# Second layer's attention: TensorE's order written out in the source instead of found by the planner

## The chip, the cores and the metric

The kernel runs on one core of one Trainium2 chip. The core has five engines that run side by side, each through its own list of instructions in order: TensorE (PE in the profile; matmuls, results in PSUM), VectorE (DVE), ScalarE (ACT), GpSimd (POOL) and SyncE (SP, which only issues DMA transfers here). They wait for each other through semaphores. The metric is the device time of one execution in microseconds; less is better. Before the change it was 1603.55 us (median of 3 runs, 1603.0 to 1605.21).

## The reference: what is computed

Two transformer layers over 512 latent tokens and 256 context tokens of width 1024, in float32. The change touches the attention of the second layer, where only the latent tokens are still updated:

```python
h_x = modulate(rmsnorm(x, norm_g[1, 0]), shift, scale);  h_c = ...            # 512 x 1024, 256 x 1024
q_x, k_x, v_x = split(h_x @ w_in_c, [1024, 1280])      # 16 query heads of 64, 4 key and value heads
k_c, v_c      = split(h_c @ w_in_c[:, 1024:], 2)
q_x, k_x      = rope(q_x), rope(k_x)
# each block of 128 queries sees 256 context keys and the latent keys within 128 positions:
s = q @ k.T / 8, masked;  p = softmax([s, sink])[..., :-1];  o = p @ v        # sink: one learned logit per head
x = x + gate * (o @ w_out_c)                                                   # 1024 x 1024
```

After it come the norm and the SwiGLU feed-forward part of the layer, and the last norm.

## The kernel before

**Layout.** Activations lie with features on the 128 partitions and tokens along the free axis: eight tiles `hb[k]` (views `hx` for the 512 latent, `hc` for the 256 context tokens). Every float32 product is made of three fast ones: each operand is split into a high and a low part (`split`, L196 and L197), and `mm3` (L207 to L209) issues high x high, high x low and low x high for each of the `KT` = 8 blocks of the contraction, 24 matmuls of 512 columns for a projection of 128 outputs.

**Weights** come through `Stream` (`S`): SP loads a 512 KB tile, ScalarE makes its high part (L158), VectorE its low part (L159). `S.next()` hands out the next in a fixed order and asks for those after it; there are three buffers of each kind.

**The stage.** Its PSUM pools are two buffers of two banks for scores (`sps`, tile `s`), one bank for projections (`linp`, tile `lin`) and three banks for everything else (`tp`, tile `t`). First come keys 0 (`k_x(0)`), the norm of the context (`rstd_of`, `h_make`), the values (`v_part`, matmuls L432 to L434 of 256 columns), context keys and keys 1, then query tile 0 (`q_piece(0)`). A query tile goes through `q_tile`: `rope_of` reads the projection's bank twice on VectorE (L386, L387) and works twice on POOL (L388, L389), then `evac_pair` splits it on ScalarE and VectorE (L369, L372).

**The steps.** There are 32, `gqa_step(m, i)`: head pair `m` (0 to 7), block of 128 queries `i` (0 to 3). Part `a` issues the scores of both heads against context and latent keys (L1540, L1542; 512 keys for `i` 0 and 3, 640 for 1 and 2), then for each head the mask with the row's minimum on VectorE (L1544), the exponential on ScalarE (L1549, L1551), the reciprocal of the sum on VectorE (L1553, L1554) and the scaling on POOL (L1557). Part `b` turns the probabilities on TensorE (L1569, L1581: 8 or 10 transposes of 128 x 128), copies them out of PSUM (L1577 ScalarE, L1575 VectorE, L1582 ScalarE) and, at every second step, multiplies them with the values for two query blocks at once (`values`, L411, 20 to 24 matmuls) and splits the result into the place where the output projection reads it.

**Fillers.** `run_steps` (L439) traces a step's `a`, the last step's `b`, then that step's fillers: whole query projections (`q_piece`, 24 matmuls) and first halves of the output projection (`first_part`, 12 matmuls per 128 outputs, over head pairs 0 to 3), listed by `plan` (L1636). After the 32 steps, `wo1` adds the second halves.

**What sets the order.** The source order is not the order on the engines. A planner runs the traced instructions through a timeline of its own at build time, and puts on each engine's list the instruction that is ready first by that timeline, with the source order as priority; at run time each list is worked off in order. `high_priority` and `issue_after` in `unbroken` (L396) keep one group of matmuls together as far as the planner lets them.

Of the kernel before, what the change touches and what calls it, by code (L numbers as in the profile page):

```python
# [11 lines left out]
ALU = mybir.AluOpType  # L12
# [5 lines left out]
KT = D // P  # L18
NX = 512
# [18 lines left out]
def tile_trunk(  # L38
# [27 lines left out]
    nc = tc.nc  # L66
# [138 lines left out]
    def mm3(ps, wh, wl, xh, xl, n=KT):  # L205
        for k in range(n):
            nc.tensor.matmul(ps, wh(k), xh(k), start=k == 0, stop=False)  # L207
            nc.tensor.matmul(ps, wh(k), xl(k), start=False, stop=False)  # L208
            end = nc.tensor.matmul(ps, wl(k), xh(k), start=False, stop=k == n - 1)  # L209
        return end  # L210
# [1242 lines left out]
    with ExitStack() as st:  # L1453
# [18 lines left out]
        def q_tile(m, ps):  # L1472
            qs[m] = gp.tile([P, 2, NX], F32R, tag="gq", name="gq", bufs=4)
            evac_pair(qs[m], 0, NX, rope_of(ps, gp), -0.125)


        def k_x(i, w):
            ps = tp()
            mm3(ps, *w, xh, xl)
            evac_pair(k1[:, 2 * i : 2 * i + 2, :], NC, NX, rope_of(ps, gp), 1.0)  # L1480
# [7 lines left out]
        def v_part(g, w):  # L1488
            ps = tp((P, 2, 256))
            v_group(ps, g, w)  # L1490
            nc.scalar.copy(v[:, 2 * g : 2 * g + 2, :], ps)

        w0 = [wslice(t) for t in S.next()]
        k_x(0, w0)
        r = rstd_of(linp(), c_sums, D, npool)
# [29 lines left out]
        def gqa_step(m, i):  # L1525
            kv = m // 2
            lo, hi = max(i - 1, 0), min(i + 1, 3)
            nk = (hi - lo + 1) * P
            d = {}

            def a():
                q = qs[m]
                small = lambda name: gp.tile([P, 2], F32, tag=name, name=name, bufs=4)
                mx, rs, es = small("mx"), small("rs"), small("es")
                pp = []
                for c in range(2):
                    ql = q[:, c, i * P : (i + 1) * P]
                    s = sps.tile([P, 1024], F32, tag="s", name="s")
                    for n, k in ((0, k1), (1, k2)):
                        nc.tensor.matmul(s[:, 256:512], ql, k[:, kv, 0:NC], start=(n == 0), stop=(n == 1))  # L1540
# [3 lines left out]
                    nc.vector.tensor_tensor_reduce(  # L1544
                        out=sv, in0=sv, in1=gm0 if i == 0 else gm[:, 0 : 256 + nk], op0=ALU.add, op1=ALU.min,
                        scale=1.0, scalar=snk[:, 2 * m + c : 2 * m + c + 1], accum_out=mx[:, c : c + 1],
                    )
                    p = gp.tile([P, 640], F32, tag="p", name="p", bufs=5)
                    nc.scalar.activation(p[:, 0 : 256 + nk], sv, AF.Exp, bias=mx[:, c : c + 1], scale=-1.0, accum_out=rs[:, c : c + 1])  # L1549
# [3 lines left out]
                nc.vector.tensor_add(rs, rs, es)  # L1553
                nc.vector.reciprocal(rs, rs)  # L1554
                for c in range(2):
                    z = pp[c][:, 0 : 256 + nk]
                    nc.gpsimd.tensor_scalar(z, z, rs[:, c : c + 1], 1.0, op0=ALU.mult, op1=ALU.mult)  # L1557
                d["p"] = pp

            def b():  # L1560
                nb = 2 + hi - lo + 1
                h = i % 2
                if h == 0:
                    turned[0] = gp.tile([P, 2, 10, P], F32, tag="pt", name="pt", bufs=1)
                pt = turned[0]
                for c in range(2):
                    t = tp((P, 4, P))
                    for k in range(4):
                        nc.tensor.transpose(t[:, k, :], d["p"][c][:, k * P : (k + 1) * P], ident)  # L1569
                    if i == 0:  # L1570
                        z, t = pt[:, c, 0:6, :].rearrange("p (a b) n -> p a b n", b=3)[:, :, 0:2, :], t.rearrange("p (a b) n -> p a b n", b=2)
                    else:
                        z = pt[:, c, 5 * h : 5 * h + 4, :]
                    if c:
                        nc.vector.tensor_copy(z, t)  # L1575
                    else:
                        nc.scalar.copy(z, t)  # L1577
# [24 lines left out]
            return a, b  # L1602


        x1 = {}

        def wo1(m, w, c0, n, k0):
            wh, wl = wo_slices(w, m % 2)
            ps = tp() if k0 else linp()
            cs = slice(c0, c0 + n)  # L1610
            if k0:
                before[0] = mm3(ps[:, 0:n], wh, wl, lambda k: hx[k0 + k][:, 0, cs], lambda k: hx[k0 + k][:, 1, cs], 4)
            else:
                mm3(ps.rearrange("p (a n) -> p a n", a=2), wh, wl, lambda k: att(k)[0], lambda k: att(k)[1], 4)
            gate = mod[1][:, 2, 0, m : m + 1]
            if k0 == 0:
                x1[m] = xr[m]
            nc.vector.scalar_tensor_tensor(x1[m][:, cs], ps[:, 0:n], gate, x1[m][:, cs], op0=ALU.mult, op1=ALU.add)

        def first_part(t):  # L1620
            d = {}

            def f(m):
                if m % 2 == 0:
                    d["w"] = S.next()
                wo1(m, d["w"], 0, NX, 0)

            return [lambda m=m: f(m) for m in (2 * t, 2 * t + 1)]

        for m in range(KT):  # L1630
            S.add(wo_c[m])
        spool = []
        super_weights(1, type("", (), {"tile": lambda self, *a, **k: spool[0].tile(*a, **k)})())
        q_piece(0)()
        steps, fillers = [], []
        plan = {  # L1636
            0: [q_piece(1), q_piece(2)], 1: [q_piece(3), q_piece(4)], 2: [q_piece(5)], 3: [q_piece(6)], 4: [q_piece(7)],
            5: first_part(0), 6: first_part(1) + first_part(2), 7: first_part(3),
        }
        for m in range(8):  # L1640
            steps += [gqa_step(m, i) for i in range(4)]
            fillers += spread(plan[m], 4)
        run_steps(steps, fillers)
        held = []
        for t in range(4):
            w = S.next(0 if t >= 2 else 2)
            for m in (2 * t, 2 * t + 1):
                if t == 0:
                    wo1(m, w, 0, NX, 4)
                else:  # L1650
                    wo1(m, w, 0, 256, 4)
                    held.append((m, w))


        halves = [slice(0, 256), slice(256, 512)]
        sums = sq_sum([x1[k][:, halves[0]] for k in range(KT)], npool)
        for m, w in held[:1]:
            wo1(m, w, 256, 256, 4)
        r = rstd_of(tp(), sums, D, npool)
        for k in range(KT):  # L1660
            h_make(k, hc[k], x1[k][:, halves[0]], r, 1, 1, 0, npool)
        for m, w in held[1:]:
            wo1(m, w, 256, 256, 4)
# [319 lines left out]
```

## Time and profile before

| | |
|---|---|
| median of 3 runs | 1603.55 us |
| span of the profiled execution | 1606.8 us |
| TensorE busy in the span | 1541.8 us (96%), 9854 matmuls |
| VectorE, ScalarE, POOL busy | 1242.9 (77%), 734.1 (46%), 275.9 (17%) us |
| HBM traffic over the span | 103 GB/s |

Times within the execution are counted from the span's start. The stage of the change begins near 990 us and hands over to the feed-forward part near 1240 us. A row of the timeline gives start, duration, engine, line, operation, output and inputs, shape and count, and in square brackets the idle time of the engine just before and what ended it. The duration of a matmul holds its way through the array, so successive ones overlap, and the distance of their starts is what one costs. In rows of windows each engine's busy time is followed by its number of instructions; behind the last engine stand the granted clock of TensorE (1.00 is full speed), the share of the DMA engines and the GB/s they moved. In rows of groups stand busy time, mean duration in ns, and the idle time before them with what ended it.

### The profile page before, as it was taken

What the parts mean: (1) busy time and instruction counts of PE and PEld (TensorE: products, weight loads), DVE (VectorE), ACT (ScalarE), POOL (GpSimd) and SP (SyncE); (2) the same over time, 40 slices, a digit from 0 to 9 for tenths busy, and PEclk for the clock granted to TensorE, in tenths of its full rate; (3) what the DMA queues carried; (4) which work ended last, traced back from release to release, by engine and by line L of the source; (5) the groups of instructions that cost most, each with busy time, mean ns of one, the idle gap of its engine ahead of it and who ended that gap; (6) DMA issues with size and microseconds to landing.
All of it is one profiled execution on the core that took longest, in us unless ns stands there. A gap on an engine that the chain in (4) does not pass through costs nothing.

```text
span 1606.8 us, 25479 instructions
## 1 busy us (share of the span) xinstructions
PE 1541.8 (96%) x9854; PEld 1377.4 (86%) x9854; DVE 1242.9 (77%) x2125; ACT 734.1 (46%) x1276; POOL 275.9 (17%) x311
## 2 busy tenths in 40 slices
PE   5899999999999999999999999999998999999997
PEld 3798888877878998999999998886777899989897
DVE  4667798966698789879798867677766987869686
ACT  4346545445344413434424254466664543525354
POOL 2222223463010000010100001354331000000001
PEclk9999999999999999999999999999999999999999
DMA  9312354543145465485866652320011442423321
GB/s 348 100 53 70 99 157 136 182 128 101 63 132 158 118 173 155 133 221 154 213 183 162 201 146 71 106 66 27 15 40 54 131 144 68 131 72 100 118 80 53
DMA packets 68577, 195.28 MB, mean 122 GB/s; under 512 B 6772, under 2 KB 19220, under 8 KB 68456
## 3 DMA queue, kind: packets, MB, share of 16 engines
q1 hardware_dynamic: 58824, 161.26, 31.5%
q0 software_dynamic: 9056, 31.87, 9.4%
q8 instruction: 78, 1.28, 0.3%
q10 hardware_dynamic: 576, 0.52, 0.1%
q14 instruction: 43, 0.35, 0.1%
HBM read 160.45 MB, written 4.86 MB: 103 GB/s over the span
## 4 chain that ended last, share of the span: by engine, by line
PE 52%; DVE 5%; DMA 4%; issue 4%; ACT 1%; POOL 0%; DVEq 0%; POOLq 0%; ACTq 0%; SPq 0%
PE f L1764 4%; PE f L1763 4%; PE f L1762 4%; PE f L1334 4%; PE f L1333 4%; PE f L1332 4%; PE f L1374 3%; PE f L1375 3%; PE f L1373 3%; PE t L411 2%; PE f L1815 2%; PE f L1817 2%; PE f L1816 2%; DMA wl<-raw 2%; PE t L1569 2%
## 5 line engine op out<-in xcount | busy, mean ns | idle before, releaser
L196 ACT ACTIVATE wh<-raw 128x1024 fp32r<-128x1024 f32 (+1 forms) x96 | 92.3, 978 | 232.4 <-DVE raw L540 106.6
L207 PE MATMUL lin<-hb,wh 128*128 128x512 f32 (+1 forms) x456 | 162.1, 356 | 8.3 <-DVE rbuf L387 2.1
L208 PE MATMUL lin<-hb,wh 128*128 128x512 f32 (+1 forms) x456 | 160.3, 351 | 1.0 <-DVE hb L1106 0.7
L209 PE MATMUL lin<-hb,wl 128*128 128x512 f32 (+1 forms) x456 | 158.4, 347 | 0.0
L197 DVE TENSOR_TENSOR wl<-raw,wh 128x1024 fp32r<-128x1024 f32 (+1 forms) x96 | 107.1, 1122 | 36.3 <-ACT wh L196 34.3
L269 DVE SCALAR_TENSOR_TENSOR junk<-raw,tables 128x1024 bf16<-128x1024 f32 x80 | 98.6, 1233 | 19.2 <-DMA raw<-in_ada_wT_dram 18.7
L202 POOL DMA_DIRECT2D wl<-raw x39 | 34.0, 872 | 445.3 <-ACT wl L201 412.0
L207 PEld LDWEIGHTS lin<-hb,wh 128*128 128x128 f32 x456 | 86.3, 189 | 23.9 <-issue 2.8
L1373 PE MATMUL f<-g,wh 128*128 128x512 f32 (+1 forms) x304 | 103.0, 340 | 0.6 <-DVE s L1362 0.6
L1374 PE MATMUL f<-g,wh 128*128 128x512 f32 (+1 forms) x304 | 102.9, 339 | 0.0
L1763 PE MATMUL f<-hb,wh 128*128 128x256 f32 x360 | 101.8, 284 | 0.0
L1762 PE MATMUL f<-hb,wh 128*128 128x256 f32 x360 | 101.6, 283 | 0.0
L1764 PE MATMUL f<-hb,wl 128*128 128x256 f32 x360 | 101.4, 284 | 0.0
L1375 PE MATMUL f<-g,wl 128*128 128x256 f32 (+1 forms) x304 | 100.8, 337 | 0.0
L1334 PE MATMUL f<-hb,wl 128*128 128x384 f32 x288 | 96.5, 335 | 1.0 <-DMA wl<-raw 1.0
L208 PEld LDWEIGHTS lin<-hb,wh 128*128 128x128 f32 x456 | 86.5, 190 | 12.4 <-DVE hb L1106 1.4
L159 DVE TENSOR_TENSOR wl<-raw,wh 128x1024 fp32r<-128x1024 f32 x61 | 80.7, 1325 | 20.6 <-ACT wh L158 20.3
L1332 PE MATMUL f<-hb,wh 128*128 128x384 f32 x288 | 96.4, 335 | 0.0
L1333 PE MATMUL f<-hb,wh 128*128 128x384 f32 x288 | 96.4, 335 | 0.0
L209 PEld LDWEIGHTS lin<-hb,wl 128*128 128x128 f32 x456 | 86.5, 190 | 10.8
L158 ACT CAST wh<-raw 128x1024 fp32r<-128x1024 f32 x61 | 63.9, 1048 | 67.0 <-PE t L208 15.0
L339 POOL TENSOR_TENSOR ns_a<-ns_a,ns_s 128x256 f32<-128x256 f32 (+1 forms) x16 | 17.9, 1118 | 433.7 <-ACT ns_s L335 427.0
(395 smaller groups left out, 4851.3 us busy)
## 6 DMA issues: line engine op xcount, KB each, us to landing
raw<-in_w_dram SPq DMA_DIRECT2D x132, 512.0 KB, 3.7
raw<-in_ada_wT_dram SPq DMA_DIRECT2D x80, 512.0 KB, 3.8
wl<-raw POOLq DMA_DIRECT2D x39, 512.0 KB, 6.3
raw<-in_w_ab_dram SPq DMA_DIRECT2D x24, 512.0 KB, 4.2
raw<-in_ada_w_dram SPq DMA_DIRECT2D x16, 512.0 KB, 9.5
raw<-in_w_c_dram SPq DMA_DIRECT2D x12, 512.0 KB, 4.4
nb<-in_na_bias_dram POOLq DMA_DIRECT2D x16, 256.0 KB, 3.2
raw<-in_wo_ab_dram SPq DMA_DIRECT2D x8, 512.0 KB, 3.7
```

Source lines behind the costliest of these rows:

```text
L207: nc.tensor.matmul(ps, wh(k), xh(k), start=k == 0, stop=False)
L208: nc.tensor.matmul(ps, wh(k), xl(k), start=False, stop=False)
L209: end = nc.tensor.matmul(ps, wl(k), xh(k), start=False, stop=k == n - 1)
L1332: nc.tensor.matmul(ps, wh(k), b[:, 0, :], start=k == 0, stop=False)
L1333: nc.tensor.matmul(ps, wh(k), b[:, 1, :], start=False, stop=False)
L1334: nc.tensor.matmul(ps, wl(k), b[:, 0, :], start=False, stop=k == 3)
L1373: nc.tensor.matmul(ps, hi, g[:, 0, cols[v]], start=first, stop=False)
L1374: nc.tensor.matmul(ps, hi, g[:, 1, cols[v]], start=False, stop=False)
L1375: nc.tensor.matmul(ps, lo, g[:, 0, cols[v]], start=False, stop=last)
L1762: nc.tensor.matmul(ps, wh(k), b[:, 0, :], start=k == 0, stop=False)
L1763: nc.tensor.matmul(ps, wh(k), b[:, 1, :], start=False, stop=False)
L1764: nc.tensor.matmul(ps, wl(k), b[:, 0, :], start=False, stop=k == 3)
```

## The change

From ahead of `k_x(0)` until after the squares for the next norm, TensorE's instructions are put on its list in the order of the source; the other engines' lists are still made by the planner. The source order is rewritten for it. A projection is cut into parts that keep one PSUM bank between them: a query tile into 3 + 3 + 2 of its 8 blocks (9, 9 and 6 matmuls), a first half of the output projection into 2 + 2 of its 4 (6 matmuls each). That makes 21 parts of queries 1 to 7, spread over steps 0 to 17, and 16 of the output projection, spread over steps 18 to 31: one part per step, two at steps 0, 6, 12, 18 and 25. Part `b` of a step is divided into turnings (`b`) and values (`b2`). For step n the order is: its scores, the turnings of step n - 1, the filler part, the values of step n - 1 (if it is an odd one). Query tile 0 is still whole and stands directly ahead of the first scores. `wo1` loses its two cases; what it computes is the same.

```diff
+        def in_parts(begin, ps, h, l, cuts, done, cols=slice(0, NX), n=KT):
+            d = {}
+            def f(c):
+                if c == 0:
+                    d["w"], d["ps"] = begin(), ps()
+                o, (wh, wl) = d["ps"][:, cols], d["w"]
+                for k in range(cuts[c], cuts[c + 1]):
+                    nc.tensor.matmul(o, wh(k), h(k), start=k == 0, stop=False)
+                    nc.tensor.matmul(o, wh(k), l(k), start=False, stop=False)
+                    nc.tensor.matmul(o, wl(k), h(k), start=False, stop=k == n - 1)
+                if c == len(cuts) - 2:
+                    done(d["ps"])
+            return [lambda c=c: f(c) for c in range(len(cuts) - 1)]
...
+        by_hand = st.enter_context(ExitStack())
+        by_hand.enter_context(tc.manual_schedule(engines={mybir.EngineType.PE}))
         w0 = [wslice(t) for t in S.next()]
         k_x(0, w0)
         r = rstd_of(linp(), c_sums, D, npool)
...
         def q_piece(m):
-            def f():
-                wh, wl = (wslice(t) for t in S.next())
-                ps = linp() if m else tp()
-                mm3(ps, wh, wl, xh, xl)
-                q_tile(m, ps)
-            return f
+            return in_parts(
+                lambda: [wslice(t) for t in S.next()], linp if m else tp, xh, xl, (0, 3, 6, KT), lambda ps: q_tile(m, ps)
+            )
...
                     nc.scalar.copy(pt[:, :, 5 * h + 4, :], t[:, 0:2, :])
+
+            def b2():
+                h = i % 2
                 if h == 0:
                     return
+                pt = turned[0]
                 o = tp()
...
-            return a, b
+            return a, b, b2
...
+            return [
+                f for m in (2 * t, 2 * t + 1)
+                for f in in_parts(
+                    lambda m=m: begin(m), lambda: linp().rearrange("p (a n) -> p a n", a=2),
+                    lambda k: att(k)[0], lambda k: att(k)[1], (0, 2, 4), lambda ps, m=m: done(m, ps), slice(0, 2), 4,
+                )
+            ]
...
-        q_piece(0)()
-        steps, fillers = [], []
-        plan = {
-            0: [q_piece(1), q_piece(2)], 1: [q_piece(3), q_piece(4)], 2: [q_piece(5)], 3: [q_piece(6)], 4: [q_piece(7)],
-            5: first_part(0), 6: first_part(1) + first_part(2), 7: first_part(3),
-        }
-        for m in range(8):
-            steps += [gqa_step(m, i) for i in range(4)]
-            fillers += spread(plan[m], 4)
-        run_steps(steps, fillers)
+        for f in q_piece(0):
+            f()
+        steps = [gqa_step(m, i) for m in range(8) for i in range(4)]
+
+        fillers = spread([f for m in range(1, 8) for f in q_piece(m)], 18) + spread([f for t in range(4) for f in first_part(t)], 14)
+        for n, (a, b, b2) in enumerate(steps + [(lambda: None,) * 3]):
+            a()
+            if n:
+                steps[n - 1][1]()
+            for f in fillers[n] if n < len(fillers) else []:
+                f()
+            if n:
+                steps[n - 1][2]()
...
         sums = sq_sum([x1[k][:, halves[0]] for k in range(KT)], npool)
+        by_hand.close()
         for m, w in held[:1]:
```

More of the change, by code (lines that the diff above doesn't have):

```diff
@@ L1600, in b, with add_x1, wo1, begin @@
                 split(*(z[:, i // 2, :] for z in att(m)), o[:, both])
-            return a, b
+            return a, b, b2
         x1 = {}
-        def wo1(m, w, c0, n, k0):
+        def add_x1(m, cs, ps):
+            gate = mod[1][:, 2, 0, m : m + 1]
+            nc.vector.scalar_tensor_tensor(x1[m][:, cs], ps, gate, x1[m][:, cs], op0=ALU.mult, op1=ALU.add)
+        def wo1(m, w, c0, n):
             wh, wl = wo_slices(w, m % 2)
-            ps = tp() if k0 else linp()
+            ps = tp()
             cs = slice(c0, c0 + n)
[L1611 to L1618, printed above, removed]
+            before[0] = mm3(ps[:, 0:n], wh, wl, lambda k: hx[4 + k][:, 0, cs], lambda k: hx[4 + k][:, 1, cs], 4)
+            add_x1(m, cs, ps[:, 0:n])
         def first_part(t):
             d = {}
-            def f(m):
+            def begin(m):
                 if m % 2 == 0:
                     d["w"] = S.next()
-                wo1(m, d["w"], 0, NX, 0)
-            return [lambda m=m: f(m) for m in (2 * t, 2 * t + 1)]
+                return wo_slices(d["w"], m % 2)
+            def done(m, ps):
+                x1[m] = xr[m]
+                add_x1(m, slice(0, NX), ps.rearrange("p a n -> p (a n)"))
+            return [
[5 more added lines that the diff above has]
+            ]
         for m in range(KT):
@@ L1648, in tile_trunk @@
                 if t == 0:
-                    wo1(m, w, 0, NX, 4)
+                    wo1(m, w, 0, NX)
                 else:
-                    wo1(m, w, 0, 256, 4)
+                    wo1(m, w, 0, 256)
                     held.append((m, w))
@@ L1656, in tile_trunk @@
         sums = sq_sum([x1[k][:, halves[0]] for k in range(KT)], npool)
+        by_hand.close()
         for m, w in held[:1]:
-            wo1(m, w, 256, 256, 4)
+            wo1(m, w, 256, 256)
         r = rstd_of(tp(), sums, D, npool)
@@ L1662, in tile_trunk @@
         for m, w in held[1:]:
-            wo1(m, w, 256, 256, 4)
+            wo1(m, w, 256, 256)
         nmap = PoolMap(
```

## The prediction

> **What bounds the kernel now.** I read the page first, then the engines' busy time by stages, the groups of TensorE instructions in the stage of the second attention, and then single instructions of that stage in order of time.
>
> ```profile
> span 1606.8 us, 25479 instructions
> PE 1541.8 (96%) x9854; PEld 1377.4 (86%) x9854; DVE 1242.9 (77%) x2125; ACT 734.1 (46%) x1276; POOL 275.9 (17%) x311
> ```
>
> TensorE (PE) is busy 96% of the span, so only what keeps it waiting, or slows its clock, can be won. The next rows are stretches of the stage; after the four engines' busy times comes the granted clock.
>
> ```profile
> 992.00:994.00 2.00, 2.00 (x10) 1.86 (x9) 2.00 (x4) 1.07 (x2) 0.00 (x0) 0.59 0.22 86
> ...
> 1098.00:1102.00 4.00, 1.76 (x10) 1.07 (x8) 3.94 (x11) 3.31 (x9) 1.28 (x1) 0.95 0.00 0
> 1102.00:1106.00 4.00, 3.69 (x12) 2.89 (x13) 3.29 (x9) 1.78 (x7) 3.43 (x3) 0.50 0.43 126
> ...
> 1142.00:1188.00 46.00, 46.00 (x309) 37.36 (x308) 32.20 (x71) 26.15 (x67) 15.49 (x18) 1.00 0.12 35
> ...
> 1030.00:1216.63 186.63, 175.96 (x1145) 139.51 (x1143) 134.28 (x304) 113.65 (x285) 77.58 (x80) 0.98 0.14 42
> ```
>
> In the stage TensorE idles 186.63 - 175.96 = 10.7 us. From 1142 to 1188, where projection work is still at hand, it idles not at all; from 1098 to 1102, where the list of pieces has a hole, it is busy for 1.76 of 4 us, and the four microseconds after run at half clock. Who ends these waits is in the groups:
>
> ```profile
> L1540 PE MATMUL s<-gk,gq 128*128 128x256 f32 x128 | 30.2, 319 | 7.9 <-ACT p L1549 7.3 <-DVE gq L372 0.5
> L1569 PE MATMUL t<-ident,p 128*128 128x128 f32 x256 | 35.8, 281 | 0.4 <-POOL p L1557 0.2
> ```
>
> 7.3 us are scores (L1540) that wait for a PSUM buffer which the exponential (ACT, L1549) still reads. The turnings (L1569) wait for almost nothing: the planner put projection work ahead of them.
>
> **The change part by part.** No instruction is added or dropped; 1145 matmuls of the stage get a new order. Times below are those of the profiled execution; its span of 1606.8 us is 3.2 us above the median of the runs, 1603.55 us, and I add the difference found to the median. The loads of projection weights stay in their order on SP's queue, one tile in about 14 us, with DMA engines at a share of 0.14: I cost them at nothing, and they would cost up to one landing, some 4 us, if a tile were asked for too late. POOL issues no DMA here.
>
> *Step 1, the head.* The block starts ahead of the first key projection.
>
> ```profile
> 990.39 0.51 PE L207 MATMUL t<-hb,wh 128*128 128x512 f32 x1 [1.49 <-ACT hb L354]
> 994.96 1.43 PE L312 MATMUL lin<-res,ones 128*128 128x256 f32 x4
> 998.11 0.42 DVE L317 TENSOR_SCALAR ns_v<-lin 128x256 f32<-128x256 f32 x1
> 999.03 0.40 PE L207 MATMUL t<-hb,wh 128*128 128x512 f32 x1
> 999.27 0.40 PE L432 MATMUL t<-wh,hb 128*128 128x256 f32 x2
> 999.50 0.40 PE L208 MATMUL t<-hb,wh 128*128 128x512 f32 x1
> 1001.76 0.75 DVE L355 SCALAR_TENSOR_TENSOR hb<-norm,mod,hb 128x512 fp32r<-128x512 f32 x1
> 1024.95 0.28 PE L207 MATMUL t<-hb,wh 128*128 128x256 f32 x1
> 1027.82 0.40 PE L207 MATMUL t<-hb,wh 128*128 128x512 f32 x1
> 1033.29 0.39 PE L207 MATMUL lin<-hb,wh 128*128 128x512 f32 x1
> 1038.50 0.39 PE L209 MATMUL lin<-hb,wl 128*128 128x512 f32 x1
> 1039.37 0.51 PE L1540 MATMUL s<-gk,gq 128*128 128x256 f32 x2 [0.48 <-DVE gq L372]
> ```
>
> VectorE delivers the eight normalised tiles hb one by one, the last at 1001.76 + 0.75 = 1002.5. Today value matmuls (L432 to L434) run between those of the key projection (L207 to L209). In source order the key projection comes alone: its 24 matmuls, at (1038.50 - 1033.29) / 23 = 0.227 us each, need 5.4 us and are stretched over the 12 us of deliveries. The context's norm (L312, L317 and two like it of 0.42 us on VectorE) moves behind, which can bring the last tile 1.3 us sooner: 1001.2. Then TensorE still owes 3 matmuls (0.7), the norm's four (1.1), 144 value and 48 context-key matmuls at (1027.82 - 1024.95) / 24 = 0.12 us (23.0), and the second key and first query projection (10.9): 35.7 us, so query 0 ends at 1036.9, not 1033.29: +3.7. Half-idle TensorE loses its clock: after the 1.49 us of idle at 990 it ran four microseconds at a mean of 0.58, which is 1.7 us lost. Paid at the end of this head, it makes +5.4. Bounds: 2.7 (a further 1 us off the deliveries, no clock lost) to 6.7 (no tile sooner).
>
> *Step 2, the first scores.* They need query 0 turned and split (VectorE, POOL, ScalarE, VectorE): 1039.37 - 1033.29 = 6.1 us today, under which query 1 ran, 5.4 us.
>
> ```profile
> 1027.44 1.29 POOL L389 TENSOR_TENSOR rt<-rt,ru 128x512 f32<-128x512 f32 x1
> 1035.78 2.15 POOL L389 TENSOR_TENSOR rt<-rt,ru 128x512 f32<-128x512 f32 x1
> ```
>
> Source order has nothing to put there: query 1's parts stand behind the scores, so TensorE waits bare. POOL's addition took 2.15 us there and 1.29 elsewhere, so the wait is 5.2 to 6.1; I take 5.6. The first scores start 4.9 us later than today (5.4 - 0.5), query 1's 5.4 us are still owed, and the clock is lost again (1.7). Head in all: **+12.0** (7.2 to 13.8).
>
> *Step 3, what is removed.* From the first scores to the output projection's first matmul pass 1216.56 - 1039.37 = 177.2 us. The regular stretch gives the work itself, starts being differences of rows:
>
> ```profile
> 1163.46 1.09 PE L1569 MATMUL t<-ident,p 128*128 128x128 f32 x8
> 1164.31 0.48 PE L1540 MATMUL s<-gk,gq 128*128 128x256 f32 x2
> 1165.57 0.39 PE L207 MATMUL lin<-hb,wh 128*128 128x512 f32 x1
> 1168.33 1.04 PE L1569 MATMUL t<-ident,p 128*128 128x128 f32 x8
> 1169.34 0.48 PE L1540 MATMUL s<-gk,gq 128*128 128x256 f32 x2
> 1170.38 0.40 PE L207 MATMUL lin<-hb,wh 128*128 128x512 f32 x1
> 1173.22 2.17 PE L411 MATMUL t<-pt,gv 128*64 128x256 f32 x20
> 1175.32 1.09 PE L1569 MATMUL t<-ident,p 128*128 128x128 f32 x8
> ...
> 1216.56 0.51 PE L207 MATMUL t<-hb,wh 128*128 128x512 f32 x1
> ```
>
> Turnings 0.85 or 1.01, scores 1.26 (640 keys) or 1.04 (512), a dozen projection matmuls 2.80, values 2.10. For 32 steps: 29.8 + 36.8 + 16 x 2.10 + 20 x 2.80 = 156.2 us. What is over, **-21.0**, is idle time, half clock and small waits; at least the 10 us of shown idle and 2 at half clock should go (-12).
>
> *Step 4, what is late next.* The 7.3 us on ScalarE's buffers go, since turnings and a piece now stand between two scores. In exchange the turnings of a step come right behind the next scores, with the piece behind them. One step's way through softmax:
>
> ```profile
> 1173.46 2.42 POOL L1557 TENSOR_SCALAR p<-p,rs 128x512 f32<-128x512 f32 x2 [2.35 <-DVE rs L1554]
> ...
> 1188.03 0.48 PE L1540 MATMUL s<-gk,gq 128*128 128x256 f32 x2
> 1188.91 0.88 DVE L1544 CUSTOM_DVE_ANT_0 s<-s,gm,snk 128x640 f32<-128x640 f32 x1
> 1189.92 0.59 ACT L1577 COPY pt<-t 128x512 f32<-128x512 f32 x1 [1.41 <-PE t L1569]
> 1190.40 0.80 ACT L1549 ACTIVATE p<-s,mx 128x640 f32<-128x640 f32 x1
> 1191.62 0.81 ACT L1549 ACTIVATE p<-s,mx 128x640 f32<-128x640 f32 x1
> 1192.91 0.15 DVE L1553 TENSOR_TENSOR rs<-rs,es 128x2 f32<-128x2 f32 x1
> 1193.47 1.57 POOL L1557 TENSOR_SCALAR p<-p,rs 128x640 f32<-128x640 f32 x2 [4.68 <-DVE rs L1554]
> ```
>
> Here the preceding step's turnings lie right behind the scores, as in the new order, and ScalarE's copy of them (0.59) goes ahead of the exponential. POOL ends at 1195.04; four turnings (0.43) can run before its second half is needed, so they may start 6.6 us after the scores did, or 6.0 without the copy. With 512 keys: 1169.34 to 1173.46, and POOL's pair at 0.69 each, less 0.43, is 5.1, or 5.6 with the copy. In the new order TensorE comes to these turnings after scores, turnings, piece and next scores, and after an odd step there are no values between: 1.26 + 0.85 + piece + 1.2 for 640 keys, 1.04 + 1.01 + piece + 1.0 for 512. A piece is 6 matmuls (1.44 us) or 9 (2.12), so 4.75 or 5.4, and 4.5 or 5.2. With the middles, 6.3 and 5.35, TensorE waits 1.55 us at five odd steps, 0.9 at two, 0.85 at three, 0.2 at four, and 1.9 at the last: 14.7 us. Even steps have 2.1 us of values between and wait for nothing. Behind the waiting turnings stand the piece, the values and the scores after next, so nothing on TensorE passes them. Weight splits and rotations of 1.2 to 1.5 us on VectorE will hit some odd steps; I take **+16** (8 where the shorter ways hold and VectorE is freer, 25 where every second odd step is hit).
>
> *Step 5, pieces.* The single projection bank: 21 query parts over 18 steps put query 5's last part and query 6's first into step 12, back to back, so the second waits for VectorE's two reads (about 1.5). Twelve more breaks between kinds cost about 0.08 each (2.80 less 12 x 0.227). **+2.5** (1 to 4).
>
> Sum: 12.0 - 21.0 + 16 + 2.5 = +9.5 us, so 1603.55 + 9.5 = **1613 us**. Ends: 7.2 - 21.0 + 8 + 1 = -4.8 (1599) and 13.8 - 12 + 25 + 4 = +30.8 (1634).
>
> The Trainium skill, page "TensorE: Matmul & The Clock Gate", section "HAM oscillation — how this bites in real kernels", has as its abstract rule "no PE-idle gaps >~3.4µs"; shorter gaps would leave the clock alone. The trace disagrees: 2.2 us of idle, in pieces, within 1098 to 1102 were followed by clock 0.50. By that rule the head's first loss of clock would not be, and the sum would be 1611 us; only the bare wait of step 2 would cost one.
>
> **The rivals.**
>
> *Faster: softmax keeps up.* If the way through softmax is under 4.5 us for 512 keys and 4.75 for 640, step 4 is nothing: 12.0 - 21.0 + 2.5 = -6.5, 1597 us. For it: waits for turnings are 0.2 us today, and VectorE has time (134.28 of 186.63 us). Against it: no row shows a way so short, and the planner hid it behind a dozen matmuls.
>
> *Much slower: the clock.* If each wait of about 1.5 us takes the clock down for four microseconds, as after 1098, some seven such waits cost 1.7 us each beyond the sum: +12, 1625 us. For it: the rows at 992 and 1102. Against it: the waits are single and stand 9 us apart.
>
> *No change.* Gains and waits cancel, or the new order is in effect the planner's: 1603.5 us. The value matmuls at 999.27, between those of a projection that stands ahead of them in the source, speak against the latter.
>
> **How the numbers follow.** The forecast has 0.52 (its own range 1607 to 1620), the clock 0.15, softmax keeping up 0.20, no change 0.13. A measurement of this kernel tells about 0.2% (3.2 us) from nothing. So faster 0.20, same 0.13, slower 0.67. The range, 1597 to 1631, takes in the faster rival's point and all but the end of the upper bound.
>
> **What would show it.** Right: between 990 and 1003 the key projection's matmuls with idle between them and no value matmul; a bare wait of 5 to 6 us ahead of the first scores; idle time ahead of L1540 by ACT nearly gone and 10 us or more ahead of the turnings, from POOL, at odd steps. Wrong: turnings that hardly wait, so that the stage from first scores to output projection takes about 165 us; or a planner that moves exponentials ahead of copies and shortens the way through softmax by the 0.6 us.

## The result, and the profile after

The changed kernel takes **1668.79 us** (median of 4 runs, 1666.67 to 1670.63); the kernel before, run beside it, took 1604.38 us (1603.0 to 1607.79). The ratio is **1.0395**, with a 95% interval of 1.038 to 1.041: 64 us slower, where 9.5 us slower had been forecast. The profiled execution has a span of 1666.7 us, 59.9 us more than that of before. From the page of the kernel after, the span, the busy time of the engines, TensorE's busy tenths and its clock in 40 slices:

```profile
span 1666.7 us, 25490 instructions
PE 1567.4 (94%) x9854; PEld 1390.3 (83%) x9854; DVE 1245.3 (75%) x2125; ACT 732.2 (44%) x1276; POOL 270.8 (16%) x311
PE   5999999989999999999999998888788999999997
PEclk9999999999999999999999989889898999999999
```

The same 9854 matmuls take 25.6 us more of busy time and leave 34.3 us more idle. Both lie in slices 24 to 31 (a slice is 41.7 us; the clock falls below nine tenths in 24, 26, 27, 29 and 31), the head and the steps of the attention. Stretches of the kernel after, first the key projection k_x(0), then the whole stage from the first scores to the output projection's first matmul:

```profile
985.90:1000.10 14.20, 11.18 (x27) 6.31 (x26) 13.00 (x20) 6.87 (x10) 1.15 (x2) 0.64 0.24 80
1040.91:1275.30 234.39, 194.50 (x1128) 148.44 (x1128) 130.92 (x294) 108.31 (x280) 71.85 (x78) 0.89 0.09 26
```

The second stretch in the kernel before:

```profile
1039.37:1216.56 177.19, 167.00 (x1104) 132.41 (x1105) 127.91 (x294) 110.22 (x280) 74.14 (x78) 0.98 0.11 34
```

The stage grew from 177.2 to 234.4 us, +57.2, nearly all of the loss. Its idle time went from 177.19 - 167.00 = 10.2 to 39.9 us (+29.7). The clock, summed over stretches of 2 us as busy time times what is lacking to full clock, cost 3.1 us before and 21.5 after (+18.4). Query 1, which the kernel before computed ahead of the first scores, adds 5.4. Some 4 us are left that these three don't hold. What TensorE waits for in that stage of the kernel after (total us, times, longest):

```profile
PE t L1585 <- POOL p L1573: 34.4, 15, 4.3
PE s L1556 <- ACT p L1565: 1.6, 3, 0.8
PE lin L1486 <- DVE rt L387: 1.5, 1, 1.5
```

and in the kernel before:

```profile
PE s L1540 <- ACT p L1549: 7.3, 10, 1.3
PE t L1569 <- POOL p L1557: 0.2, 1, 0.2
```

The waits of the scores for the exponential are nearly gone, as planned. In their place the turnings (now L1585) wait 34.4 us for POOL's scaling (L1573), fifteen times, all but one of them at odd steps (the last step twice, once for each head).

**Why POOL is that late.** One of the four longest of these waits, single instructions of the kernel after in order of time (start, duration, engine, line):

```profile
1112.92 0.52 PE L1558 MATMUL s<-gk,gq 128*128 128x384 f32 x2
1113.20 0.89 DVE L1560 CUSTOM_DVE_ANT_0 s<-s,gm,snk 128x640 f32<-128x640 f32 x1
1114.00 0.16 DVE L1569 TENSOR_TENSOR rs<-rs,es 128x2 f32<-128x2 f32 x1
1114.08 0.88 DVE L1560 CUSTOM_DVE_ANT_0 s<-s,gm,snk 128x640 f32<-128x640 f32 x1
1114.89 1.68 DVE L159 TENSOR_TENSOR wl<-raw,wh 128x1024 fp32r<-128x1024 f32 x1
1116.49 0.15 DVE L1570 RECIPROCAL rs<-rs 128x2 f32<-128x2 f32 x1
1116.84 3.98 POOL L1573 TENSOR_SCALAR p<-p,rs 128x640 f32<-128x640 f32 x4 [1.35 <-ACT gq L369]
1117.69 2.32 PE L1585 MATMUL t<-ident,p 128*128 128x128 f32 x8 [4.26 <-POOL p L1573]
```

The turnings at 1117.69 belong to the step before the scores at 1112.92. On VectorE that step's sum is ready at 1114.16, but its reciprocal (L1570) stands behind the second mask (L1560) of the *next* step and behind a split of weights (L159), and runs at 1116.49. POOL starts only then, and TensorE, whose list has these turnings next, stands for 4.26 us. VectorE's list is still the planner's, and the planner put the reciprocal there at build time: in 11 of the 32 steps it stands behind both masks of the next step, and four of these have a weight split in between as well. These eleven steps hold eleven of the fifteen waits, of 1.80 us and more; the other four are of 0.44, 0.72, 1.97 and 0.97 us, the latter two at the last step. The more common case, without the split, from the same kernel:

```profile
1099.49 0.76 DVE L1560 CUSTOM_DVE_ANT_0 s<-s,gm,snk 128x512 f32<-128x512 f32 x1 [0.46 <-PE s L1558]
1100.17 0.16 DVE L1570 RECIPROCAL rs<-rs 128x2 f32<-128x2 f32 x1
1100.50 1.36 POOL L1573 TENSOR_SCALAR p<-p,rs 128x512 f32<-128x512 f32 x2 [5.58 <-DVE rs L1570]
1101.25 0.33 PE L1585 MATMUL t<-ident,p 128*128 128x128 f32 x1 [1.80 <-POOL p L1573]
```

Here the mask cannot start until the next step's own scores are there, so the turnings wait for the scores that TensorE has just finished, the second mask, the reciprocal and POOL.

**What the clock does behind these waits.** Stretches of two microseconds of the kernel after, around the two waits shown; the third figure from the right is the granted clock:

```profile
1100.00:1102.00 2.00, 0.74 (x5) 0.51 (x6) 0.96 (x5) 1.01 (x4) 1.36 (x2) 0.97 0.00 0
1102.00:1104.00 2.00, 2.00 (x7) 1.81 (x8) 0.76 (x2) 0.53 (x1) 1.36 (x2) 0.50 0.00 0
1104.00:1106.00 2.00, 2.00 (x7) 1.39 (x6) 0.00 (x0) 0.00 (x0) 0.00 (x0) 0.68 0.00 0
1106.00:1108.00 2.00, 2.00 (x21) 1.28 (x20) 0.00 (x0) 0.00 (x0) 0.00 (x0) 1.00 0.00 0
...
1115.00:1117.00 2.00, 0.00 (x0) 0.00 (x0) 1.94 (x6) 1.98 (x8) 0.65 (x2) 0.63 0.00 0
1117.00:1119.00 2.00, 1.22 (x5) 0.82 (x6) 1.97 (x2) 0.59 (x2) 2.00 (x3) 0.50 0.63 170
1119.00:1121.00 2.00, 2.00 (x8) 1.90 (x9) 1.07 (x2) 0.80 (x2) 1.82 (x2) 0.50 0.23 92
1121.00:1123.00 2.00, 2.00 (x7) 1.54 (x6) 0.00 (x0) 0.00 (x0) 0.00 (x0) 0.66 0.00 0
```

A wait of 1.80 us (with 0.79 idle just ahead of it) and one of 4.26 are both followed by about four microseconds at half clock, in which the projection's matmuls begin 0.43 us apart (1120.66, 1121.09, 1121.52) instead of 0.23 (1122.60, 1122.83). Not every wait is followed by that. Behind the waits of 0.44 and 0.72 us the granted clock stays at 1.00, and so it does behind one of 2.13:

```profile
1191.16 1.33 PE L1585 MATMUL t<-ident,p 128*128 128x128 f32 x8 [2.13 <-POOL p L1573]
```

There the projection's matmuls begin 0.23 us apart (1192.56, 1192.79, 1193.03). The other twelve waits are followed by half clock, or fall into it (0.97 us, right behind the one of 1.97).

### The profile page after: what moved, and what is told of

Read it like the earlier page. It is cut to its first block, busy times and chain, and to the rows that moved or that the text cites. A ratio compares the mean times of both kernels' runs of the same rounds, so it can differ in the third digit from the quotient of the medians.

```text
span 1666.7 us, 25490 instructions
## 1 busy us (share of the span) xinstructions
PE 1567.4 (94%) x9854; PEld 1390.3 (83%) x9854; DVE 1245.3 (75%) x2125; ACT 732.2 (44%) x1276; POOL 270.8 (16%) x311
## 5 line engine op out<-in xcount | busy, mean ns | idle before, releaser
L207 PE MATMUL lin<-hb,wh 128*128 128x256 f32 (+1 forms) x368 | 126.6, 345 | 7.7 <-DVE k L380 2.2
L208 PE MATMUL lin<-hb,wh 128*128 128x256 f32 (+1 forms) x368 | 125.2, 340 | 0.9 <-DVE hb L1106 0.6
L209 PE MATMUL lin<-hb,wl 128*128 128x256 f32 (+1 forms) x368 | 123.6, 336 | 0.0
L159 DVE TENSOR_TENSOR wl<-raw,wh 128x1024 fp32r<-128x1024 f32 x61 | 81.7, 1340 | 22.6 <-ACT wh L158 22.1
L207 PEld LDWEIGHTS lin<-hb,wh 128*128 128x128 f32 x368 | 69.6, 189 | 19.7 <-DVE k L380 2.9
L208 PEld LDWEIGHTS lin<-hb,wh 128*128 128x128 f32 x368 | 69.7, 189 | 9.6 <-DVE hb L1106 1.3
L1585 PE MATMUL t<-ident,p 128*128 128x128 f32 x256 | 44.0, 313 | 35.3 <-POOL p L1573 34.4
```

## The experiments

Line numbers shift by a few between kernels; the names stay. All times are medians, ratios are to the kernel before run on the same chip beside them.

### The reciprocal ahead of the next masks

TensorE's list stays as in the changed kernel. On VectorE the masks of a step are kept behind the reciprocal of the step before.

```diff
-                    nc.vector.tensor_tensor_reduce(...)
+                    with tc.issue_after(recip[0].ins) if recip[0] else nullcontext():
+                        nc.vector.tensor_tensor_reduce(...)
...
-                nc.vector.reciprocal(rs, rs)
+                recip[0] = nc.vector.reciprocal(rs, rs)
```

> Source order on TensorE stays as in the changed kernel; on VectorE a step's mask is issued behind the last step's reciprocal (in the changed kernel the planner put one or both masks of the next step, and four times a weight split too, ahead of it). Theory Q (the long waits are made by VectorE's list): idle ahead of the turnings falls from 34.4 us to about 15, what the softmax way of 6.3 us leaves uncovered at odd steps, and TensorE's clock loses some 10 us less, so about 1640 us against 1668.8. Theory G (the source order leaves too little work ahead of the turnings, whatever VectorE does): idle stays within 5 us of 34 and the time within 6 us of 1669.

Measured: 1637.95 us, ratio 1.020 (1.0185 to 1.0215). From the waits of TensorE:

```profile
PE t L1587 <- POOL p L1575: 16.2, 15, 2.1
```

31 us of the 64 are gone by this one edit: the turnings' wait falls by 18.2 us and the clock's loss in the stage from 21.5 to 8.8. TensorE's list is the same in both kernels, so the late reciprocal is a cause and not only a thing seen. The 16.2 us that stay are the wait which the written order leaves with the reciprocals in time. Ten of these waits are of 0.44 to 0.92 us, with the granted clock at 1.00 behind each. The 8.8 us lost to the clock lie behind the head's bare wait (3.0), two of the three waits of about 2 us, and the last step.

### Filling matmuls in the wait

Nine matmuls that nobody reads are issued ahead of the turnings of every odd step (144 in all, which the trace records as 288 of 128 columns), so that TensorE works while it waits.

```diff
                     t = tp((P, 4, P))
+                    if h and c == 0:
+                        for _ in range(9):
+                            nc.tensor.matmul(t[:, 0, :], ident, ones, start=True, stop=True)
```

> Nine idle-filling matmuls of 128 columns (about 0.22 us each, 2.0 us) are issued ahead of the turnings of every odd step, into the bank that the turnings overwrite; nothing else is changed. Theory C (half clock after the waits costs some 18 of the 64 us): the clock in the stage rises from 0.89 to 0.97 or more; the filling lies in the waits but for three or four odd steps that do not wait (7 us), so about 1658 us. If the clock costs nothing, the filling can only lengthen: 1669 to 1678 us.

Measured: 1659.90 us, ratio 1.0339 (1.0319 to 1.036). The groups of TensorE in the stage show the filling and the turnings:

```profile
L1588 PE MATMUL t<-ident,p 128*128 128x128 f32 x256 | 37.7, 284 | 11.2 <-POOL p L1573 10.2
L1586 PE MATMUL t<-ones,ident 128*128 128x128 f32 x288 | 34.7, 275 | 0.0
```

More work made the kernel 8.9 us faster. The stage went from 234.4 to 228.0 us: 23 us less idle time, 14.2 us less lost to the clock (21.5 to 7.3), and about 31 us of filling on top. So the clock's loss hangs on the waits, and it is a cost beside them.

### The projection part ahead of the turnings

The two lines of the step's order are exchanged: scores, part, turnings of the last step, values of the last step.

```diff
             a()
-            if n:
-                steps[n - 1][1]()
             for f in fillers[n] if n < len(fillers) else []:
                 f()
             if n:
+                steps[n - 1][1]()
                 steps[n - 1][2]()
```

> Order of a step: scores, projection part, turnings of the last step, its values (part and turnings exchanged). Theory Q and theory G both say that 1.4 to 2.1 us more stand ahead of the turnings: idle there falls from 34 us to under 10, and with no wait over 1.1 us the clock stays up. The values now stand right behind the turnings and wait for the copies out of PSUM, about 1 us at 16 steps. About 1638 us. If it stays at 1660 or more, the waits only move to the values.

Measured: 1646.08 us, ratio 1.025 (1.0233 to 1.0266), 8 us above the expectation. The waits show why:

```profile
PE t L1585 <- POOL p L1573: 11.1, 8, 2.8
PE t L411 <- DVE pt L1591: 9.9, 12, 1.1
PE t L411 <- DVE rs L1569: 3.5, 2, 1.7
```

The turnings wait 23 us less. The values (L411), which now follow the turnings at once, wait about 14 us, 9.9 of them for VectorE's copies of what was turned. The part can stand in one of the two gaps only.

### The head left to the planner

The written order begins at step 0, and query 1 moves ahead of the steps; 18 parts of queries 2 to 7 instead of 21 are left for steps 0 to 17.

```diff
-        by_hand = st.enter_context(ExitStack())
-        by_hand.enter_context(tc.manual_schedule(engines={mybir.EngineType.PE}))
         w0 = [wslice(t) for t in S.next()]
...
-        for f in q_piece(0):
+        for f in q_piece(0) + q_piece(1):
             f()
+        by_hand = st.enter_context(ExitStack())
+        by_hand.enter_context(tc.manual_schedule(engines={mybir.EngineType.PE}))
```

> The written order begins only after the second query tile: keys, values and query tiles 0 and 1 are left to the planner; query tiles 2 to 7 (18 parts) go over steps 0 to 17. The head of my prediction was 12 us: key projection at the pace of its inputs 4, bare wait of 5.9 us ahead of the first scores with query 1 still owed 5.4, clock 2 to 4. So about 1657 us. If the head costs nothing, 1669 us.

Measured: 1663.18 us, ratio 1.035 (1.0328 to 1.0372). The head falls from 53.4 to 48.95 us and query 1 (5.4) is in it, but only 5.6 of these 9.8 us reach the end by the medians (7 by the ratios, whose intervals leave some 4 us either way, so that the shortfall is not certain). The turnings' wait grew to 38.6 us, in seventeen waits instead of fifteen. Steps 0, 6 and 12 now hold one part where they held two, and VectorE's list was planned again too (12 reciprocals behind both masks instead of 11); no run separates the two, though with the reciprocals in time the wait grows as well (16.2 to 18.8 us, next section).

### Head and reciprocal together

> Two edits together: the planner orders TensorE as far as query 1 and the written order begins at step 0 (as in e4_head), and VectorE's list has every step's reciprocal ahead of the next step's masks (as in e1_recip). Theory that the two costs lie in different stages and add: 1637.95 of e1_recip less the head's 4.4 us and query 1's 5.4 us that the head then does in its idle time = 1628 us. Rival, that the head's gain is partly eaten because the steps lose the three parts of query 1 that stood ahead of turnings (e4_head gave back 4.2 of 9.8 us so): 1632 us. In both the wait of the turnings for GpSimd's scaling stays at 16 to 20 us.

Measured: 1628.14 us, ratio 1.0145 (1.0129 to 1.016). Within the noise the costs add: with the reciprocals in time the head gives 9.8 us by the medians and 8.8 by the ratios. The turnings wait 18.8 us.

### Part ahead of the turnings, with the reciprocal

> e1_recip's VectorE order, and in every step the projection part ahead of the last step's turnings (as in e3_first). Theory that a wait only moves when the work ahead of it is only exchanged: the turnings' 16.2 us of wait falls to 1 or 2 us, the values, which now follow the turnings at once, wait 10 to 14 us for the copies of the turned tile; what is saved is a few us of clock: 1633 us (1629 to 1638). Rival, that the turnings' wait was the only cost left: 1637.95 - 16 - 5 (clock) = 1617 us.

Measured: 1635.88 us, ratio 1.0196 (1.0182 to 1.021). The wait moves as expected, though the turnings keep 4.5 us where 1 or 2 were expected:

```profile
PE t L411 <- DVE pt L1593: 12.1, 14, 1.1
PE t L1587 <- POOL p L1575: 4.5, 3, 2.8
```

### Values a step later, with the reciprocal

Each step: its scores, the values of the step before the last, the part, the turnings of the last step. So the part stands ahead of the turnings, and the next scores stand between turnings and values.

```diff
-        for n, (a, b, b2) in enumerate(steps + [(lambda: None,) * 3]):
+        for n, (a, b, b2) in enumerate(steps + 2 * [(lambda: None,) * 3]):
             a()
-            if n:
-                steps[n - 1][1]()
+            if n > 1:
+                steps[n - 2][2]()
             for f in fillers[n] if n < len(fillers) else []:
                 f()
-            if n:
-                steps[n - 1][2]()
+            if 0 < n <= len(steps):
+                steps[n - 1][1]()
```

> e1_recip's VectorE order, and on TensorE the order of a step is: its scores, the values of the step before the last one, its projection part, the turnings of the last step. So a part stands between scores and turnings, and the scores of a whole step stand between a turned tile's copies and the values that read it. Theory that the order's loss lies in what the program puts between producer and reader, and nothing else: turnings' and values' waits together under 4 us, clock lost under 5 us, 1637.95 - 16 - 5 = 1617 us (1613 to 1622). Rival, that TensorE is held by VectorE's and GpSimd's own load whatever the order: waits of over 10 us remain, at the scores or the turnings, and the time is over 1628 us.

Measured: 1614.04 us, ratio 1.0057 (1.0044 to 1.0069). From the waits of TensorE, the first of them being the head's bare one:

```profile
PE s L1557 <- DVE gq L372: 5.9, 1, 5.9
PE s L1557 <- ACT p L1567: 4.5, 7, 1.5
PE t L1587 <- POOL p L1575: 0.9, 1, 0.9
```

Turnings and values together wait 3.7 us, and the clock's loss in the stage is 3.0 us, no more than in the kernel before; all of it lies behind the head's bare wait. VectorE and POOL are fast enough; what was missing is work between producer and reader.

### The same order, reciprocals left to the planner

> e7_lagv_recip's order on TensorE, but VectorE's list is left to the planner, which again puts the reciprocal behind one or both masks of the next step in 15 of 32 steps. Theory that the late reciprocal costs only where nothing but the next scores stands ahead of the turnings: with a part there as well (3.3 us of work between scores and turnings for a lateness of about 2 us) most of the lateness is covered, the turnings wait 3 to 8 us instead of 34.4, and the time is 1614.0 + 3 to 10 (wait and clock) = 1617 to 1624 us. Rival, that the reciprocal's place is a cost of its own: 34.4 - 16.2 = 18 us and some 12 us of clock return, 1640 us or more.

Measured: 1614.85 us, ratio 1.0071 (1.0059 to 1.0083), below the expected range and not told apart from the run with the reciprocals in time (1614.04, run against other runs of the kernel before: 1.0057, 1.0044 to 1.0069). VectorE's list, planned again for this order, has 11 reciprocals behind a mask of the next step, not the 15 of the expectation, and only 4 of them behind both, one with a weight split in between (11 and 4 in the changed kernel). The turnings hardly wait:

```profile
PE t L1585 <- POOL p L1573: 3.4, 4, 2.0
```

So the two causes do not add: the reciprocal's place costs 31 us where only the next scores stand ahead of the turnings, and nothing that can be measured in this order. Two things differ here, though: a part stands ahead of the turnings, and the planner left fewer reciprocals behind both masks. Whether the part alone would cover a list as late as the changed kernel's was not run.

### All of it: reciprocal, order, head

> e7_lagv_recip, with the planner ordering TensorE as far as query 1 as well (as in e4_head). Theory that the causes named (reciprocal behind the masks, order of turnings and values, head, clock behind the waits) are the whole of the change's loss: 1617 - 4.4 (head) - 5.4 (query 1) = 1607 us (1603 to 1613), no slower than the kernel before within 0.5%. Rival, that a part of the loss is in the order by the program itself: 1615 us or more.

Measured: 1606.41 us (11 runs), ratio 1.0009 (1.0000 to 1.0018), not slower by more than 0.2%. The stage and its largest wait:

```profile
1037.30:1213.42 176.12, 164.79 (x1104) 132.98 (x1104) 126.72 (x294) 106.96 (x280) 73.44 (x78) 0.95 0.11 35
```

```profile
PE s L1555 <- ACT p L1565: 8.6, 10, 2.2
```

The loss is accounted for, but the written order wins nothing either: the stage is 1.1 us shorter than the planner's 177.2 in one execution of each, with no gain in the time, and it still idles 11.3 us, most of it at the scores again.

### Parts given out unevenly

The version with all the edits, but with pieces cut by single weight tiles, three to one for steps without values.

```diff
-                lambda: [wslice(t) for t in S.next()], linp if m else tp, xh, xl, (0, 3, 6, KT), lambda ps: q_tile(m, ps)
+                lambda: [wslice(t) for t in S.next()], linp if m else tp, xh, xl, tuple(range(KT + 1)), lambda ps: q_tile(m, ps)
...
-        fillers = spread([...], 18) + spread([...], 14)
+        def uneven(items, n):
+            w = [3 if k % 2 == 0 else 1 for k in range(n)]
+            ends = [round(len(items) * sum(w[: k + 1]) / sum(w)) for k in range(n)]
+            return [items[i:j] for i, j in zip([0] + ends, ends)]
+        fillers = uneven([...], 18) + uneven([...], 14)
```

> e8_lagv_all, with the projection pieces cut by single weight tiles and given out three to one to the steps that have no values and those that have them, so that the work between two steps' scores is more even (5.2 and 3.9 us on average there, now 3.9 and 5.9). e8_lagv_all's scores wait 8.6 us for the exponentials, ten times, mostly in steps without values. Theory that these waits come from the uneven work: they fall to 3 or 4 us, 1606.4 - 5 = 1601 us. Rival, that they come from evictions and weight splits that stand ahead of the masks and exponentials on ScalarE's and VectorE's lists: they stay at 7 to 10 us, 1605 to 1608 us.

(The averages in that expectation are mixed up: with even parts the steps with values have the 5.9 us of work and those without the 3.9.) Measured: 1615.19 us, ratio 1.0067 (1.0055 to 1.0079). The waits:

```profile
PE s L1555 <- ACT p L1565: 8.4, 6, 2.4
PE lin L1486 <- DVE res L1629: 5.6, 6, 1.2
PE lin L1486 <- DVE rt L387: 4.8, 4, 1.4
```

The scores' wait did not fall, as the rival said, but neither theory had the new cost. With bunched parts a piece ends and the next begins in one step, and there is one bank for both: the first matmul of the new one waits for VectorE's reads of the old, 10.4 us in all. That is the wait which the prediction's step 5 saw once, at step 12, and which this edit made ten times.

### The runs together

| TensorE's order | reciprocals | head | us | stage, us | turnings' wait | clock's loss in the stage |
|---|---|---|---|---|---|---|
| planner's (before) | planner's | planner's | 1604.4 | 177.2 | 0.2 | 3.1 |
| the change | planner's | written | 1668.8 | 234.4 | 34.4 | 21.5 |
| the change, waits filled | planner's | written | 1659.9 | 228.0 | 10.2 | 7.3 |
| the change | planner's | planner's | 1663.2 | 231.3 | 38.6 | 20.1 |
| the change | in time | written | 1638.0 | 204.2 | 16.2 | 8.8 |
| the change | in time | planner's | 1628.1 | 200.3 | 18.8 | 7.3 |
| part first | planner's | written | 1646.1 | 210.2 | 11.1 | 9.9 |
| part first | in time | written | 1635.9 | 202.8 | 4.5 | 7.0 |
| values a step later | planner's | written | 1614.9 | 182.6 | 3.4 | 3.3 |
| values a step later | in time | written | 1614.0 | 180.5 | 0.9 | 3.0 |
| values a step later | in time | planner's | 1606.4 | 176.1 | under 0.4 | - |
| the same, parts uneven | in time | planner's | 1615.2 | 186.3 | under 0.4 | 1.6 |

Waits and clock are those of the profiled execution. The stage runs from the first scores to the output projection's first matmul; with the head left to the planner it holds 5.4 us less work. The clock of the execution without a figure is the subject of the last section.

## Why the prediction was wrong, point by point

**Step 1 and 2, the head: right.** Single instructions of the kernel after:

```profile
987.55 0.50 PE L207 MATMUL t<-hb,wh 128*128 128x512 f32 x1 [1.49 <-ACT hb L354]
...
995.41 0.79 PE L208 MATMUL t<-hb,wh 128*128 128x512 f32 x1 [0.81 <-DVE hb L355]
...
1040.91 0.80 PE L1556 MATMUL s<-gk,gq 128*128 128x256 f32 x2 [5.85 <-DVE gq L372]
```

The key projection is stretched over 12.5 us, and the stretch shown above has clock 0.64. The bare wait is 5.85 us, within the 5.2 to 6.1. From its first matmul to the first scores the head takes 1040.91 - 987.55 = 53.4 us instead of 49.0: +4.4, where +4.9 was worked out, and query 1 is still owed. The run with the head left to the planner, once the reciprocals are in time, gives 1637.95 - 1628.14 = 9.8 us back by the medians, against 12.0 predicted with the clock in it.

**Step 3, what is removed: mis-sized, -21.0 us where hardly anything came.** The waits on ScalarE's buffers did go (7.3 to 1.6 us). But the 156.2 us of "the work itself", taken from a few differences of starts in the best stretch, are below what any order here came to. In the planner's order its busy time at full clock is 167.00 x 0.98 = 163.7 us, and the uneven variant, at clock 0.99, has the same:

```profile
1033.27:1219.58 186.31, 165.38 (x1105) 130.06 (x1105) 128.09 (x294) 108.80 (x280) 73.09 (x78) 0.99 0.11 32
```

that is 165.38 x 0.99 = 163.7. By this reckoning 177.2 - 163.7 = 13.5 us were to be had, not 21.0, and no order tried here had more than some 2 us of them (180.5 less query 1's 5.4 is 175.1 us, in the run with the values a step later and the reciprocals in time). In the changed kernel idle time other than the turnings' fell from 10.0 to 5.5 us, and the 4 us without a name took that back.

**Step 4, the waits of the turnings: the step that failed.** It named the right wait, at the right steps (fourteen of the fifteen waits are at odd ones), and put it at 16 us (8 to 25). It was 34.4. The way through softmax was read from the old trace, where the reciprocal follows its sum at once (1192.91 and POOL at 1193.47), and I let that stand for the new kernel. But only TensorE's list was written by hand. VectorE's was planned again, and nothing in the old trace had fixed the reciprocal's place in it. The old trace even held a warning: in five of its 32 steps the reciprocal stands behind both masks of the next step, once 2.3 us behind its sum, with a weight split in between:

```profile
1100.60 0.16 DVE L1553 TENSOR_TENSOR rs<-rs,es 128x2 f32<-128x2 f32 x1
1103.09 0.15 DVE L1554 RECIPROCAL rs<-rs 128x2 f32<-128x2 f32 x1
```

There two heads' scores and three projection matmuls still ran before the turnings, which waited 0.2 us. Collisions with weight splits were counted as an occasional 1.2 to 1.5 us; they came four times, each as part of a wait of 3.3 to 4.3. With the reciprocals held in time, the list that the step assumed, the same term measures 16.2 us in fifteen waits. The total is right, but with some luck: of the five steps put at 1.55 us none came out so, three odd steps waited about 2.0 us, most others 0.7 to 0.9, and the last 2.9.

**Step 5, pieces: right where it can be read.** The wait of the one projection bank is 1.5 us, once.

**The rival of the clock was real, and larger than priced.** I gave it +12 us and a chance of 0.15, and left it out of the sum, because the waits are single and 9 us apart. That reason fell: twelve of the fifteen stand before or in microseconds at half clock, which cost 1.4 to 2.3 us behind each of the longer ones. Counted over this kernel and the run with the reciprocals in time, twelve waits of 0.44 to 0.92 us left the clock at 1.00, ten of twelve of 1.80 to 2.16 us took it down, and all four of 3.26 us and more did; the two of 0.97 us fell into half clock. So here the change comes between 0.9 and 1.8 us, and around 2 us the wait's length alone does not settle it. The stage lost 18.4 us more to the clock than before, and the filled waits show that it is the waits' doing. Forecast and this rival were also not exclusive, as they were treated; here both came, at twice the waits.

**The three together.** For the stretch from the first scores to the output projection the prediction's terms make -21.0 + 16 + 2.5, query 1's 5.4 and 1.7 for the clock behind the bare wait, +4.6 us. Measured was +57.2. Of the 52.6 us between them the turnings' wait holds 18, the clock 20, and about 15 are gains of step 3 that did not come. So step 4, with the clock that hangs on its waits, is the largest cause and not the only one: with the reciprocals in time the kernel still took 1637.95 us, 25 us more than forecast.

**The Trainium skill**, page "TensorE: Matmul & The Clock Gate", section "HAM oscillation — how this bites in real kernels", asks for "no PE-idle gaps >~3.4µs". By that rule twelve of the fifteen waits (3.26 us and less) would have left the clock alone, and the loss would hang on the three of over 4 us. The trace disagrees again: eight of those twelve, of 1.80 to 3.26 us, were followed by half clock.

**Not a cause.** With the block taken away and the source's new order kept, the lists of all five engines as built are those of the kernel before, instruction for instruction. This is read from the built lists, without a run of its own; it leaves only the written order as the difference. The accounts by stage leave about 4 us of the 57 without a name: they lie in TensorE's recorded busy time, beyond the clock.

## What to carry to other kernels

Writing out one engine's order leaves the other engines' orders to be planned again, and a short instruction such as a reciprocal can then land behind work that needs the very engine that waits for it: predict from the new lists, or fix the producer's place together with the reader's. An in-order engine needs work of its own between every producer and reader pair, both of them here (scores to turnings, copies to values): one filler between two pairs only moves the wait. Where waits of 2 us recur on TensorE, price each with its clock as well: here most of them cost between half and nearly all of the wait again, and waits under 1 us nothing.

## What was not expected of the hardware

Adding 144 matmuls that nobody reads (288 in the trace), some 31 us of TensorE time, made the kernel 8.9 us faster, because they stood in waits and kept the clock up.

The profiled execution of the version with all the edits shows a granted clock near 0.95 in every stretch (0.95 in the window quoted above; 0.943 over the whole), yet its span of 1604.7 us is that of its other executions (1599.7 to 1606.4 us, at 0.992 to 0.997). So an even 0.95 over a whole execution was not time lost, unlike the 0.50 of single microseconds, and the clock column is best compared within one execution. Why the records show it is open.
